# SwiGLU blocks: the rank of the copies and sums that empty a block's four banks

## The chip, the cores and the metric

The kernel runs on one core of a Trainium2 chip. The metric is device time in microseconds; of several executions the median is taken. In the profile's words TensorE is PE (its weight loads are PEld), VectorE is DVE, ScalarE is ACT, GpSimd is POOL and SyncE, which issues the transfers, is SP. L750 is line 750 of the kernel before.

## What is computed

An encoder of two layers on 256 tokens of width 1024, in float32. Each layer has a SwiGLU half-step, an attention stage, a second SwiGLU half-step and a gated embedding. The change is in the SwiGLU half-steps. D_FF is 2816.

```python
def rms_norm(x, g):
    xf = x.astype(jnp.float32)
    y = xf * lax.rsqrt(jnp.mean(xf * xf, axis=-1, keepdims=True) + EPS) * g.astype(jnp.float32)
    return y.astype(x.dtype)

def swiglu(h, w_in, w_out):
    gate, up = jnp.split(h @ w_in, 2, axis=-1)
    return (jax.nn.silu(gate) * up) @ w_out
...
    for i in range(DEPTH):
        x = x + 0.5 * swiglu(rms_norm(x, norm_ffn1[i]), ffn1_w_in[i], ffn1_w_out[i])
...
        x = x + 0.5 * swiglu(rms_norm(x, norm_ffn2[i]), ffn2_w_in[i], ffn2_w_out[i])
...
    return x
```

## The kernel before

Every float32 operand is held as two parts, a rounded one ("hi") and the remainder ("lo"), and a product is made of three matmuls: hi by hi, hi by lo, lo by hi. Weights are loaded as raw tiles of 128x1024 (wraw, four buffers). Weights.piece casts half a tile on ScalarE to whi (L236, or L238 with the norm's gain in it), and the remainder wlo is made on VectorE (L243, L245); whi and wlo have eight buffers each. When a tile's last remainder is made, its raw buffer is free and SyncE loads the next tile.

A SwiGLU half-step (ffn) runs over eleven blocks of 256 columns, numbered 0 to 10. Block 0 is made in another way. For blocks 1 to 10, columns(j) takes four banks at once, two of the kind mm (gate), one tp and one op (up), and runs 64 matmuls over four weight tiles. Each bank holds 128 columns of the block for all 256 tokens: hi by hi in its left half, the two mixed products in its right half. Then product(j, kc), once for each half kc of the block, empties a gate bank and an up bank: ScalarE copies the left halves (L742, L744), VectorE adds the right halves (gate_sum, L750, and other_sum, L757). The gate is multiplied by 1/rms (L752), goes through silu on ScalarE (L761), times up on VectorE (L766), and is split into hi and lo (pth by L458 on ScalarE, ptl by L466 on VectorE). Behind the columns of each block, and ahead of the next block's, come output units (OUT_BEHIND, out_unit): three or four times six matmuls of 512 columns into four banks of another kind, acc. The last four output parts (OUT_LEFT) come at the end.

The order of all engines' instructions is fixed when the program is built. A planner, Pace, holds a time for each engine and adds a cost for each instruction that it places. Work that waits for a result is entered with pace.at(time, function, engine, rank). When the planner's time reaches it, it goes on the engine's list of due work, and Pace.check takes the lowest rank first. Weight remainders have rank 5; casts of weights are placed by Weights.pump whenever the planner's ScalarE and VectorE are nearly idle. Banks and scratch buffers (sq, two of them) are given back at planned times. So a change of rank moves other work too, in all later stages.

Two more steps matter below. setup (L519 to L529) prepares the table of position biases: three small VectorE operations, a matmul into an op bank (L524), its copy on VectorE (L527), and a transfer to device memory on SyncE (L529). It is due at the planner's time 30 and then waits until an sq buffer and an op bank are free. zero_pads (L548) fills the zero columns of the keys and values on ScalarE, due at 40 with rank 9. The attention stage (mixers) makes queries and keys, normalises each head (L854 to L884), turns them with four transposes into the bank tp (L438), and goes on with scores and values, in an order that the planner finds step by step.

Of the kernel before, what the change touches and what calls it, by code (L numbers as in the profile page):

```python
# [19 lines left out]
DM, S, DEPTH, HD = 1024, 256, 2, 64  # L20
# [277 lines left out]
def encoder(ctx: ExitStack, tc, ins, out):  # L298
# [14 lines left out]
    pace = Pace()  # L313
# [6 lines left out]
    def can(kind):  # L320
        return slots[kind][turn[kind]] <= pace.now
# [10 lines left out]
    def give(tile, t=0.0):  # L332

        kind, k, _ = owner.pop(id(tile))
        slots[kind][k] = t
# [5 lines left out]
    def scratch(kind):  # L341
        return take(kind, sm.tile([P, 512], F32, tag=kind, name=kind, bufs=2))
# [109 lines left out]
    def parts(hi, lo, src, n, scale=None, bank=None, then=None, ready=None, prio=1):  # L452

        cell = {}

        def high():
            if scale is None:
                nc.scalar.copy(hi, src)  # L458
            else:
                nc.scalar.activation(hi, src, AF.Copy, scale=scale)  # L460
            cell["hi"] = pace.act(n, ready, scale=scale is not None)
            pace.at(cell["hi"], low, "dve", prio)

        def low():
            if scale is None:
                nc.vector.tensor_tensor(out=lo, in0=src, in1=hi.bitcast(F32), op=ALU.subtract)  # L466
            else:
                nc.vector.scalar_tensor_tensor(out=lo, in0=src, scalar=scale, in1=hi.bitcast(F32), op0=ALU.mult, op1=ALU.subtract)
            cell["lo"] = pace.dve(n, cell["hi"], scale=scale is not None)
            if bank is not None:  # L470
                give(bank, cell["lo"])
            if then:
                then(cell["lo"])
        ready = pace.done() if ready is None else ready
        pace.at(ready, high, "act", prio)
        return cell
# [159 lines left out]
    def ffn(a, ids, first=False):  # L636
# [8 lines left out]
        def slot(j):  # L645
            if j not in hT:
                hT[j] = take_pt()
            return hT[j]
# [59 lines left out]
        def columns(j):  # L708

            kinds = ("mm", "mm", "tp", "op")  # L710
            pace.until(lambda: all(max(slots[kind]) <= pace.now for kind in kinds))
            banks = [bank(kind) for kind in kinds]
            for c in range(4):
                ks = (2 * c, 2 * c + 1)
                pace.until(lambda: all(a.cell[t][k].get("lo") for t in range(2) for k in ks))
                wh, wl = W.get(ids_in[j][c])
                r = max(W.when[ids_in[j][c]], *(a.cell[t][k]["lo"] for t in range(2) for k in ks))
                every = [(k, n) for k in ks for n in range(4)]
                step = COLUMN_GROUP
                for g in range(0, 8, step):  # L720
                    for lower in range(2):
                        for k, n in every[g:g + step]:
                            x2 = xhl[:, k, :, :].rearrange("p u q -> p (u q)")
                            o = slice(512 * (k % 2) + P * n, 512 * (k % 2) + P * (n + 1))
                            if lower:
                                mm(banks[n][:, S:], wl[:, o], x2[:, :S], False, k == KD - 1)
                            else:
                                mm(banks[n], wh[:, o], x2, k == 0, False, r)
                            pace.check()
                W.used(ids_in[j][c])  # L730
                pace.check()
            for kc in range(2):
                product(j, kc, banks[kc], banks[2 + kc])

        def product(j, kc, g_ps, u_ps):
            pace.until(lambda: can("sq") and "r" in has)
            gu = scratch("sq")
            g, u = gu[:, :S], gu[:, S:]
            p0 = pace.done()

            def gate():
                nc.scalar.copy(g, g_ps[:, :S])  # L742
                t1 = pace.act(S, p0)
                nc.scalar.copy(u, u_ps[:, :S])  # L744
                t2 = pace.act(S, p0)
                pace.at(t1, lambda: gate_sum(t1), "dve", 0)
                pace.at(t2, lambda: other_sum(t2), "dve", 1)

            def gate_sum(t1):
                nc.vector.tensor_tensor(out=g, in0=g_ps[:, S:], in1=g, op=ALU.add)  # L750
                give(g_ps, pace.dve(S, t1))
                nc.vector.tensor_tensor(out=g, in0=g, in1=rms_b, op=ALU.mult)  # L752
                t3 = pace.dve(S, has["r"])
                pace.at(t3, lambda: act(t3), "act", 1)

            def other_sum(t2):
                nc.vector.tensor_tensor(out=u, in0=u_ps[:, S:], in1=u, op=ALU.add)  # L757
                give(u_ps, pace.dve(S, t2))

            def act(t1):  # L760
                nc.scalar.activation(g, g, AF.Silu)  # L761
                t2 = pace.act(S, t1, sbuf=True)
                pace.at(t2, lambda: prod(t2), "dve", 1)

            def prod(t2):
                nc.vector.tensor_tensor(out=u, in0=u, in1=g, op=ALU.mult)  # L766
                t3 = pace.dve(S, t2)
                split(t3)

            def split(t3):  # L770
                if j not in hT and not can("pt"):
                    pace.at(pace.now + 0.1, lambda: split(t3))
                    return
                hh, hl = slot(j)
                made[j, kc] = parts(hh[:, kc, :], hl[:, kc, :], u, S, ready=t3, then=lambda end: give(gu))
            pace.at(p0, gate, "act", 1)

        def out_unit(j, kc, t):
            if not acc:
# [456 lines left out]
```

## Time and profile before

| | us |
|---|---|
| median of 3 runs | 1029.19 (1029.05 to 1029.32) |
| profiled execution | 1029.5 |
| its span | 1027.7 |

| engine | busy us | share of the span | instructions |
|---|---|---|---|
| TensorE, matmuls | 1018.9 | 99% | 5466 |
| TensorE, weight loads | 875.6 | 85% | 5466 |
| VectorE | 765.4 | 74% | 1578 |
| ScalarE | 687.7 | 67% | 1438 |
| GpSimd | 34.0 | 3% | 38 |

How to read it: the span runs from the first to the last instruction of the program; the time of the execution is a little longer. Matmuls are pipelined, so that one of 512 columns lasts some 0.39 us while the next begins 0.23 us after it: distances between starts tell more than durations. A wait is put down to the engine and line that ended it last. By the chain of waits, 88% of the span is TensorE's.

### The profile page before, as it was taken

The page shows a single profiled execution, that of the slowest core. Times are in us where ns is not written, and L with a number is a line of the kernel's source. Part 1 is how long each engine was busy: PE and PEld are TensorE (multiplying, and loading weights), DVE is VectorE, ACT ScalarE, POOL GpSimd, SP SyncE. Part 2 cuts the span into 40 slices and gives each one's busy share as a digit, 9 for nine tenths or more (in the row PEclk, how much of TensorE's full clock was granted, in tenths as well). Part 3 has the DMA queues.
Part 4 walks back from the last instruction along what each step waited for, and adds up shares of the span by engine and source line. Part 5 has one row for each costly group of instructions (what it writes and reads, how often), then busy time and mean ns, then how long its engine had stood idle before and what let it go on. Part 6 is the DMA issues. An engine that isn't in the chain of part 4 may idle for free.

```text
span 1027.7 us, 15622 instructions
## 1 busy us (share of the span) xinstructions
PE 1018.9 (99%) x5466; PEld 875.6 (85%) x5466; DVE 765.4 (74%) x1578; ACT 687.7 (67%) x1438; POOL 34.0 (3%) x38
## 2 busy tenths in 40 slices
PE   9999999999999999999999999999999999999998
PEld 7788888879888888888888888888888888888887
DVE  6685874899887757847887478578998786578575
ACT  7775764778877646736886366467788775467464
POOL 0000000120100000000000000001110000000000
PEclk9999999999999999999999999999999999999999
DMA  8655764466435536745665457536664366366261
GB/s 296 222 204 165 230 206 156 147 230 209 150 119 201 177 114 211 234 150 170 235 193 180 145 172 258 165 132 209 206 195 132 120 208 219 102 228 231 97 207 62
DMA packets 55911, 187.30 MB, mean 182 GB/s; under 512 B 6502, under 2 KB 10854, under 8 KB 55832
## 3 DMA queue, kind: packets, MB, share of 16 engines
q1 hardware_dynamic: 55832, 186.30, 54.5%
q8 instruction: 43, 0.70, 0.3%
q14 instruction: 36, 0.29, 0.1%
HBM read 185.19 MB, written 1.08 MB: 181 GB/s over the span
## 4 chain that ended last, share of the span: by engine, by line
PE 88%; DVE 4%; ACT 3%; DMA 2%; issue 1%; POOL 1%; SPq 0%; ACTq 0%; DVEq 0%
PE acc L401 37%; PE mm L401 25%; PE op L401 12%; PE tp L401 10%; DVE wlo L245 2%; DMA wraw<-in_ffn_in_dram 2%; PE tp L438 2%; ACT whi L238 1%; POOL hrs L866 1%; PE op L438 1%; DMA wraw<-in_qkv_dram 0%; DVE kal L466 0%; PE acc L438 0%; DVE hss L862 0%; SPq L209 0%
## 5 line engine op out<-in xcount | busy, mean ns | idle before, releaser
L245 DVE SCALAR_TENSOR_TENSOR wlo<-wraw,gains,whi 128x512 fp32r<-128x512 f32 (+1 forms) x464 | 318.8, 737 | 52.7 <-ACT whi L238 49.8
L238 ACT ACTIVATE whi<-wraw,gains 128x512 fp32r<-128x512 f32 (+1 forms) x464 | 301.2, 707 | 65.2 <-DMA wraw<-in_ffn_in_dram 41.3
L401 PE MATMUL mm<-xhl,whi 128*128 128x512 f32 x640 | 200.2, 394 | 0.3 <-DVE sq L750 0.3
L243 DVE TENSOR_TENSOR wlo<-wraw,whi 128x512 fp32r<-128x512 f32 x216 | 140.3, 686 | 25.0 <-ACT whi L236 18.4
L236 ACT CAST whi<-wraw 128x512 fp32r<-128x512 f32 x216 | 124.2, 617 | 50.8 <-PE op L401 24.9
L401 PE MATMUL acc<-whi,pth 128*128 128x512 f32 x352 | 137.8, 391 | 0.0
L401 PE MATMUL acc<-wlo,pth 128*128 128x512 f32 x352 | 137.5, 390 | 0.0
L401 PE MATMUL acc<-whi,ptl 128*128 128x512 f32 x352 | 137.0, 389 | 0.0
L401 PE MATMUL mm<-xhl,wlo 128*128 128x256 f32 x640 | 127.8, 281 | 0.0
L401 PEld LDWEIGHTS mm<-xhl,whi 128*128 128x128 f32 x640 | 112.2, 189 | 17.7 <-DVE sq L750 0.9
L401 PE MATMUL op<-xhl,whi 128*128 128x512 f32 x320 | 125.5, 392 | 0.5 <-DVE sq L527 0.5
L401 PE MATMUL tp<-xhl,whi 128*128 128x512 f32 x320 | 124.6, 389 | 0.3 <-DVE sq L757 0.3
L401 PEld LDWEIGHTS mm<-xhl,wlo 128*128 128x128 f32 x640 | 110.0, 190 | 12.5
L750 DVE TENSOR_TENSOR sq<-mm,sq 128x256 f32<-128x256 f32 x80 | 33.7, 421 | 115.5 <-ACT sq L742 115.4
L401 PE MATMUL acc<-whi,xhl 128*128 128x512 f32 (+1 forms) x384 | 115.5, 373 | 0.0
L742 ACT COPY sq<-mm 128x256 f32<-128x256 f32 x80 | 30.4, 380 | 94.5 <-PE mm L401 94.5
L401 PE MATMUL op<-xhl,wlo 128*128 128x256 f32 x320 | 90.6, 283 | 0.0
L401 PE MATMUL tp<-xhl,wlo 128*128 128x256 f32 x320 | 90.5, 283 | 0.0
L401 PEld LDWEIGHTS acc<-whi,xhl 128*128 128x128 f32 x384 | 70.7, 189 | 12.3 <-ACT whi L238 0.7
L401 PEld LDWEIGHTS acc<-whi,ptl 128*128 128x128 f32 x352 | 66.1, 188 | 14.0
L401 PEld LDWEIGHTS acc<-whi,pth 128*128 128x128 f32 x352 | 66.3, 188 | 12.5
L401 PEld LDWEIGHTS acc<-wlo,pth 128*128 128x128 f32 x352 | 66.3, 188 | 12.1
(153 smaller groups left out, 1576.2 us busy)
## 6 DMA issues: line engine op xcount, KB each, us to landing
wraw<-in_ffn_in_dram SPq DMA_DIRECT2D x172, 512.0 KB, 4.4
wraw<-in_ffn_out_dram SPq DMA_DIRECT2D x88, 512.0 KB, 4.7
wraw<-in_qkv_dram SPq DMA_DIRECT2D x36, 512.0 KB, 3.6
wraw<-in_wo_dram SPq DMA_DIRECT2D x16, 512.0 KB, 3.8
wraw<-in_gate_dram SPq DMA_DIRECT2D x16, 512.0 KB, 4.1
bias<-bias_d SPq DMA_DIRECT2D x32, 192.0 KB, 3.7
wraw<-in_ffn_in_dram SPq DMA_DIRECT2D x8, 256.0 KB, 5.7
wraw<-in_ple_dram SPq DMA_DIRECT2D x4, 512.0 KB, 4.5
```

Of the source, the lines that this page charges most:

```text
L236: nc.scalar.copy(hi[:, a:b], raw[:, a:b])
L238: nc.scalar.activation(hi[:, a:b], raw[:, a:b], AF.Copy, scale=g)
L243: nc.vector.tensor_tensor(out=lo[:, a:b], in0=raw[:, a:b], in1=hi[:, a:b].bitcast(F32), op=ALU.subtract)
L245: nc.vector.scalar_tensor_tensor(out=lo[:, a:b], in0=raw[:, a:b], scalar=g, in1=hi[:, a:b].bitcast(F32), op0=ALU.mult, op1=ALU.subtract)
L401: nc.tensor.matmul(ps, lhsT=lhsT, rhs=rhs, start=start, stop=stop)
L438: nc.tensor.transpose(tp[:, n * P:(n + 1) * P], src, ident)
L742: nc.scalar.copy(g, g_ps[:, :S])
L750: nc.vector.tensor_tensor(out=g, in0=g_ps[:, S:], in1=g, op=ALU.add)
L866: nc.gpsimd.tensor_tensor(out=rs[:, :nh], in0=ss[:, :nh], in1=half_t[:, :nh], op=ALU.pow)
```

## The change

In product, three ranks change and one step is split. The first step, gate (the copies on ScalarE), goes from rank 1 to 0. The up sum goes from rank 1 to 0, the same as the gate sum. The scaling by 1/rms no longer follows the gate sum in the same step; it is a step of its own, scaled, at rank 1, entered for the time at which the sum is done.

```diff
--- before.py
+++ after.py
@@ -744,11 +744,15 @@
                 nc.scalar.copy(u, u_ps[:, :S])
                 t2 = pace.act(S, p0)
                 pace.at(t1, lambda: gate_sum(t1), "dve", 0)
-                pace.at(t2, lambda: other_sum(t2), "dve", 1)
+                pace.at(t2, lambda: other_sum(t2), "dve", 0)
 
             def gate_sum(t1):
                 nc.vector.tensor_tensor(out=g, in0=g_ps[:, S:], in1=g, op=ALU.add)
-                give(g_ps, pace.dve(S, t1))
+                end = pace.dve(S, t1)
+                give(g_ps, end)
+                pace.at(end, scaled, "dve", 1)
+
+            def scaled():
                 nc.vector.tensor_tensor(out=g, in0=g, in1=rms_b, op=ALU.mult)
                 t3 = pace.dve(S, has["r"])
                 pace.at(t3, lambda: act(t3), "act", 1)
@@ -773,7 +777,7 @@
                     return
                 hh, hl = slot(j)
                 made[j, kc] = parts(hh[:, kc, :], hl[:, kc, :], u, S, ready=t3, then=lambda end: give(gu))
-            pace.at(p0, gate, "act", 1)
+            pace.at(p0, gate, "act", 0)
 
         def out_unit(j, kc, t):
             if not acc:
```

No instruction is added or removed. Line numbers below the split grow by four: the scaling is L756 in the changed kernel, the up sum L761, the product L770.

VectorE, the end of block 1 in layer 1's first half-step (sq_431 and sq_432 are the scratch of the two halves, wlo_429 a weight remainder). Before:

```order
L750 TENSOR_TENSOR sq_431<-mm_283,sq_431 128x256
L752 TENSOR_TENSOR sq_431<-sq_431,rms_b_152 128x256
L750 TENSOR_TENSOR sq_432<-mm_284,sq_432 128x256
L752 TENSOR_TENSOR sq_432<-sq_432,rms_b_152 128x256
L757 TENSOR_TENSOR sq_431<-tp_285,sq_431 128x256
L757 TENSOR_TENSOR sq_432<-op_286,sq_432 128x256
L766 TENSOR_TENSOR sq_431<-sq_431 128x256
L766 TENSOR_TENSOR sq_432<-sq_432 128x256
L245 SCALAR_TENSOR_TENSOR wlo_429<-wraw_375,gains_89,whi_428 128x512
```

Now:

```order
L750 TENSOR_TENSOR sq_431<-mm_283,sq_431 128x256
L245 SCALAR_TENSOR_TENSOR wlo_429<-wraw_375,gains_89,whi_428 128x512
L761 TENSOR_TENSOR sq_431<-tp_285,sq_431 128x256
L750 TENSOR_TENSOR sq_432<-mm_284,sq_432 128x256
L761 TENSOR_TENSOR sq_432<-op_286,sq_432 128x256
L756 TENSOR_TENSOR sq_431<-sq_431,rms_b_152 128x256
L756 TENSOR_TENSOR sq_432<-sq_432,rms_b_152 128x256
L770 TENSOR_TENSOR sq_431<-sq_431 128x256
L770 TENSOR_TENSOR sq_432<-sq_432 128x256
L245 SCALAR_TENSOR_TENSOR wlo_429<-wraw_375,gains_89,whi_428 128x512
```

All four sums come ahead of the first scaling, and half of a weight tile's remainder has come in between. On ScalarE, the cast of that tile's second half now stands between the two silus.

TensorE, the start of block 2's columns, before (op_488 is the bank of setup's matmul):

```order
L401 MATMUL acc_436<-whi_381,pth_366 128x512
L401 MATMUL acc_436<-wlo_382,pth_366 128x512
L401 MATMUL acc_436<-whi_381,ptl_367 128x512
L524 MATMUL op_488<-qn_117,rb_116 16x512
L401 MATMUL mm_501<-xhl_151,whi_396 128x512
L401 MATMUL mm_502<-xhl_151,whi_396 128x512
L401 MATMUL tp_503<-xhl_151,whi_396 128x512
L401 MATMUL op_504<-xhl_151,whi_396 128x512
```

TensorE, the end of the output units ahead of block 5's columns, now:

```order
L401 MATMUL acc_433<-whi_855,pth_822 128x512
L401 MATMUL acc_433<-wlo_856,pth_822 128x512
L401 MATMUL acc_433<-whi_855,ptl_823 128x512
L524 MATMUL op_970<-qn_117,rb_116 16x512
L401 MATMUL acc_434<-whi_855,pth_822 128x512
L401 MATMUL acc_434<-wlo_856,pth_822 128x512
L401 MATMUL acc_434<-whi_855,ptl_823 128x512
L401 MATMUL mm_988<-xhl_151,whi_859 128x512
L401 MATMUL mm_989<-xhl_151,whi_859 128x512
L401 MATMUL tp_990<-xhl_151,whi_859 128x512
L401 MATMUL op_991<-xhl_151,whi_859 128x512
```

The setup's matmul has moved from ahead of block 2 to ahead of block 5, three matmuls before the end of the output units. Its copy (L527) moved with it on VectorE and stands behind the first of block 4's two product remainders; its transfer (L529) moved on SyncE from place 27 to place 44.

VectorE, the end of block 3's columns. Before:

```order
L245 SCALAR_TENSOR_TENSOR wlo_779<-wraw_727,gains_89,whi_778 128x512 x2
L750 TENSOR_TENSOR sq_793<-mm_668,sq_793 128x256
L752 TENSOR_TENSOR sq_793<-sq_793,rms_b_152 128x256
L750 TENSOR_TENSOR sq_794<-mm_669,sq_794 128x256
L752 TENSOR_TENSOR sq_794<-sq_794,rms_b_152 128x256
L757 TENSOR_TENSOR sq_793<-tp_670,sq_793 128x256
L757 TENSOR_TENSOR sq_794<-op_671,sq_794 128x256
L766 TENSOR_TENSOR sq_793<-sq_793 128x256
L766 TENSOR_TENSOR sq_794<-sq_794 128x256
```

Now:

```order
L245 SCALAR_TENSOR_TENSOR wlo_757<-wraw_708,gains_89,whi_756 128x512 x2
L245 SCALAR_TENSOR_TENSOR wlo_772<-wraw_723,gains_89,whi_771 128x512
L750 TENSOR_TENSOR sq_785<-mm_658,sq_785 128x256
L761 TENSOR_TENSOR sq_785<-tp_660,sq_785 128x256
L245 SCALAR_TENSOR_TENSOR wlo_772<-wraw_723,gains_89,whi_771 128x512
L750 TENSOR_TENSOR sq_786<-mm_659,sq_786 128x256
L761 TENSOR_TENSOR sq_786<-op_661,sq_786 128x256
L756 TENSOR_TENSOR sq_785<-sq_785,rms_b_152 128x256
L756 TENSOR_TENSOR sq_786<-sq_786,rms_b_152 128x256
```

The last half tile of weight remainders now comes after the first gate and up sums, and the scalings after all four sums.

In the attention stage the order of TensorE changes from the second group of head transposes on. Counted in the order, 36 matmuls stood between the first and the second group and 30 between the second and the third; now it is 39 and 36. The second layer's stage changes in the same way.

## Rows read from the trace of the kernel before

**Rows 1.** The page's first two sections: busy time of each engine; TensorE's granted clock by slices.
```profile
PE 1018.9 (99%) x5466; PEld 875.6 (85%) x5466; DVE 765.4 (74%) x1578; ACT 687.7 (67%) x1438; POOL 34.0 (3%) x38
...
PEclk9999999999999999999999999999999999999999
```

**Rows 2.** The view of waits, TensorE's weight loads: total us, times, longest us.
```profile
PEld op L401 <- DVE sq L527: 0.9, 1, 0.9
PEld mm L401 <- DVE sq L750: 0.9, 2, 0.6
...
PEld tp L401 <- DVE sq L757: 0.6, 1, 0.6
```

**Rows 3.** The chain that ended last: start us, us, what.
```profile
82.18 5.47 PE acc L401 x24
```

**Rows 4.** Timeline of TensorE, 35 to 39: start us, us, engine, line, operation.
```profile
35.47 0.39 PE L401 MATMUL acc<-whi,ptl 128*128 128x512 f32 x1
35.79 1.03 PE L524 MATMUL op<-qn,rb 34*16 34x512 f32 x2
36.74 0.73 PE L401 MATMUL mm<-xhl,whi 128*128 128x512 f32 x2
...
38.18 0.50 PE L401 MATMUL op<-xhl,whi 128*128 128x512 f32 x1 [0.47 <-DVE sq L527]
38.51 0.62 PE L401 MATMUL mm<-xhl,whi 128*128 128x512 f32 x2
```

**Rows 5.** Timeline of TensorE, 69 to 72 us.
```profile
69.25 0.39 PE L401 MATMUL acc<-whi,ptl 128*128 128x512 f32 x1
69.50 0.50 PE L401 MATMUL mm<-xhl,whi 128*128 128x512 f32 x1
...
71.09 0.50 PE L401 MATMUL tp<-xhl,whi 128*128 128x512 f32 x1 [0.29 <-DVE sq L757]
...
71.76 0.62 PE L401 MATMUL mm<-xhl,whi 128*128 128x512 f32 x2
```

**Rows 6.** Timeline of VectorE, 69 to 71 us.
```profile
69.03 0.42 DVE L750 TENSOR_TENSOR sq<-mm,sq 128x256 f32<-128x256 f32 x1
69.48 0.42 DVE L752 TENSOR_TENSOR sq<-sq,rms_b 128x256 f32<-128x256 f32 x1
...
70.62 0.42 DVE L757 TENSOR_TENSOR sq<-tp,sq 128x256 f32<-128x256 f32 x1
70.95 0.41 DVE L757 TENSOR_TENSOR sq<-op,sq 128x256 f32<-128x256 f32 x1
```

**Rows 7.** Timeline of VectorE, 37 to 39 us.
```profile
37.23 0.23 DVE L519 SCALAR_TENSOR_TENSOR gqk<-gains 128x2 f32<-128x2 f32 x2
...
37.45 0.67 DVE L527 COPY sq<-op 16x512 f32<-16x512 f32 x1
38.05 1.39 DVE L245 SCALAR_TENSOR_TENSOR wlo<-wraw,gains,whi 128x512 fp32r<-128x512 f32 x2
```

**Rows 8.** Timeline of ScalarE, 50 to 68 us.
```profile
50.11 0.40 ACT L548 CAST kbh<-zero_t 64x256 fp32r<-64x256 f32 x1
...
64.28 3.84 ACT L238 ACTIVATE whi<-wraw,gains 128x512 fp32r<-128x512 f32 x6 [0.87 <-DMA wraw<-in_ffn_in_dram]
```

**Rows 9.** Timelines of VectorE and TensorE after block 4, 84 to 88 us.
```profile
84.19 0.41 DVE L757 TENSOR_TENSOR sq<-op,sq 128x256 f32<-128x256 f32 x1
...
87.48 0.61 PE L401 MATMUL mm<-xhl,whi 128*128 128x512 f32 x2
```

**Rows 10.** Timeline of TensorE in layer 1's attention stage, 222 to 227 us.
```profile
222.37 0.39 PE L401 MATMUL mm<-whi,xhl 128*128 128x512 f32 x1
223.17 0.63 PE L438 MATMUL tp<-ident,qn 128*128 128x128 f32 x4 [0.41 <-DVE qn L884]
...
226.15 0.39 PE L401 MATMUL mm<-whi,xhl 128*128 128x512 f32 x1
226.85 0.66 PE L438 MATMUL tp<-ident,qn 128*128 128x128 f32 x4 [0.31 <-DVE qal L468]
```

## The prediction

> **What bounds the kernel now.** I read the page first, then who waits, then the timelines of the places where TensorE waits. TensorE is busy for 99% of the span, VectorE 74%, ScalarE 67%, and the granted clock is at nine tenths or more in every slice, the 2.4 GHz level [rows 1]. A busy share doesn't show that an engine is at its rate, so look at its pace: in the chain of waits 24 matmuls of 512 columns take 5.47 us [rows 3], 228 ns each, and 512 columns at 2.4 GHz are 213 ns. There is nothing to win inside such a stretch; only the places where TensorE stands still count.
>
> The change is about releasing the four banks of a block earlier. So the question is where TensorE waits for a bank. The weight loads' waits answer it [rows 2]: in the whole program TensorE waits twice for the gate sums of line 750 (0.9 us together) and once for an up sum of line 757 (0.6 us). There are 40 blocks with 160 bank releases. In the usual block, as after block 4, the last sum starts at 84.19 and takes 0.41, and TensorE comes back to these banks at 87.48 [rows 9]: almost 3 us of cover, given by the 24 output matmuls between [rows 3]. An earlier release is worth nothing there.
>
> The three waits lie at one place, at 69 to 72 us, where block 4 starts while block 3's banks are still held [rows 5]. At the pitch of 0.23 the four first matmuls would start at 69.48, and the next at 70.39; the next starts at 71.76. The stall is 1.37 us. VectorE is the cause: the first sum only starts at 69.03, then each half's sum and scaling follow in pairs [rows 6], and ahead of them ScalarE has six weight casts in one row from 64.28 [rows 8].
>
> **The change, part by part.** No operation is added or removed; each engine has the same instructions in another order. Four terms follow.
>
> 1. The setup of the bias table leaves block 2's start. The step waits for a free scratch buffer and a free op bank in the planner's time, and in the changed order it comes three blocks later. At its old place it costs TensorE directly [rows 4]: after the matmul at 35.47 the next block would start at 35.69, and its fifth matmul at 36.60. The setup runs from 35.79 to 36.74, then op waits for the copy of line 527, and the fifth matmul is at 38.51. That is 1.91 us, of which the wait is about 0.64 and restarts 0.2.
>
> 2. The same setup now stands three matmuls ahead of block 5's columns. TensorE pays its run again, 35.69 to 36.74 with the restart, 1.05 to 1.2; I take 1.1. Does op wait again? After the setup come three output matmuls, then mm, mm, tp: six times 0.23, or 1.4 us before op is wanted. The copy takes 0.67 [rows 7] and stands on VectorE just behind the first product low of that block, which is done earlier, so I take no wait; the bound above is the old 0.64, the one below 0. Behind the copy queue one weight low and the second product low; their tiles are used a block later. The step's own transfer moves on SyncE's queue as well, past 17 of its transfers; it waits for line 527, and the loads behind it wait for that same low anyhow. Nothing.
>
> 3. The stall at block 4. TensorE arrives 1.91 earlier, at 69.48 - 1.91 = 67.57, which by itself would make the wait longer. Two things work against it. First, VectorE and ScalarE come earlier too. In block 1's evacuation the weight low that starts at 38.05 had the setup's four operations (37.23 to 38.05, 0.82) ahead [rows 7], and two product lows, 0.33 each by the distance below; now it has neither, but it waits for a silu that ScalarE does one weight cast (3.84 for six, 0.64 each [rows 8]) later. Net 0.8 earlier, and the next load of weights hangs on it. One zero pad of 0.40 [rows 8] falls behind block 2's copies. So these engines run 1.1 us ahead of before at block 3; between 0 and 1.2 is possible. Second, one weight low, 0.67 (half of the 1.39 of two [rows 7], less a small overlap), goes behind the sums. The first gate sum starts at 69.03 - 1.1 - 0.67 = 67.26; then, with 0.33 between starts that don't depend on each other (70.62 to 70.95) where a sum and its own scaling are 0.45 apart (69.03 to 69.48) [rows 6], the up sum at 67.60, a weight low at 67.93, the second gate sum at 68.60 and the second up sum at 68.93, ended 69.35. TensorE: mm at 67.70, mm at 69.05, tp 69.28, op 69.51, next 69.74 against 68.48 without a wait. The stall becomes 1.26: a gain of 0.1, between a loss of 1.0 (no lead) and a gain of 1.2.
>
> 4. The attention stage, twice. Nothing of the diff is in it, but the planner's clock starts it otherwise, and its matmuls come in another order. Of the four groups of transposes of normalised heads, the third waits 0.57 (223.17, where the pitch says 222.60), the fourth 0.47 (226.85 after 226.38) [rows 10]; these are what TensorE loses at the stage's start. In the changed order the third group stands nine matmuls later, 2.0 us; VectorE has one weight low more, 0.67, ahead of it. So this wait should go. The fourth hangs on a low that frees the bank and stays. I take 0.6 off, and give half back, since a whole stage has a new order and nothing says that every new place is a lucky one: 0.3 per layer, 0.6 in all; from a gain of 1.3 to a loss of 1.0 per layer, the size of the waits in these rows.
>
> The scaling as its own step costs the product chain at most two VectorE operations, 0.7 us. Its result is used by output units after the next block's columns, or, for the last block, after three output units and two more, well over the 3 us of [rows 9]: cover enough.
>
> **Sum**: -1.91 + 1.1 - 0.1 - 0.6 = -1.5 us. The profiled execution has 1029.5 us (span 1027.7, the rest around it), so 1028.0 in its terms; the median of the runs is 1029.19, 0.3 lower, and from it the forecast is **1027.7 us**. A measurement of this kernel can tell 0.2%, 2.06 us, from no change, so this counts as no change, near the edge to faster.
>
> **Rivals.**
> - *The late engines eat it.* If VectorE and ScalarE have no lead at block 3, because the loads land when they did, the new stall is 1.0 longer, and only the better order of the sums is left: -1.91 + 1.0 + 1.1 - 0.6, or 1028.8. For it: the engines wait for loads right there. Against: those loads hang on VectorE's lows, which move forward.
> - *Attention gains in earnest.* Both waits of [rows 10] go in both layers, with the small ones after them, 1.3 each: -0.9 - 2.6, or 1025.7. For it: the third group clearly comes later. Against: the fourth waits for a bank, not for the matmul before it.
> - *Slower by a new wait in attention.* The planner places the transposes and value products where it believes the tiles ready; it knows nothing of TensorE's real 0.5 us waits. Each place that is two matmuls too early costs what [rows 10] show, 0.5. From three such places per layer (1.5 each, against the 0.9 saved before) the kernel loses; at four in each it is -0.9 + 4.0, or 1032.3. Against: the stage of before, planned by the same rules, has two.
> - *No effect.* The setup's waits come back at block 5 and the stall stays: -1.91 + 1.1 + 0.64 + 0.2, or 1029.2.
> - *TensorE isn't the bound.* The Trainium skill (Perfetto Trace Analysis, Identifying the Most-Contended Engine) holds that matmul busy time misleads and asks for the busy share of weight loads. By that rule the 85% here would leave 15%, and a prompt release could give several per cent. The mechanism in rows: matmuls would have to be further apart than their columns need; were the 0.9 us by which the last bank is free earlier (two scalings of 0.45) exposed in all 40 blocks, it would give 36 us, 993. The pace of [rows 3] speaks against it.
>
> **How the numbers follow.** Forecast 55%, spread over 1026.8 to 1028.6, a third of it below 1027.1 where faster begins; late engines 17%; attention gains 15%; slower 7%; no effect 4%; TensorE unbound 2%. Faster: 17 + 15 + 2 = 34%; same: 38 + 17 + 4 = 59%; slower 7%. The range goes from 1025.4, just past the attention case, to 1029.9, which takes in the late engines with a lost wait or two; the slower case and the last are left out. The forecast's own range is 1026.8 to 1028.6.
>
> **What would show it.** In the changed profile: no setup and no wait of op at 36 to 38 us; the setup's two passes near 84 us with no wait behind them; a stall of about 1.3 us at 67 to 70, with the first sum near 67.3; banks in all later blocks free 3 us early as before; the third group of head transposes without a wait. TensorE's waits for line 750 elsewhere, a first sum still near 68 or later, or waits of over 1 us in attention would prove the steps wrong.

## The result, and the profile after

The changed kernel takes 1034.7 us in the median of 3 runs (1034.59 to 1036.36), against 1029.19 before: a ratio of 1.0058, interval 1.0045 to 1.0072. It is slower by 5.5 us, clear of the noise. The forecast was 1027.7 with a range to 1029.9, and "slower" had 7%.

The page still shows TensorE busy for 99%, nearly the same weight loads, and less of the chain that ended last on TensorE (88% before, 80% now):

```profile
PE 1019.1 (99%) x5466; PEld 874.6 (85%) x5466; DVE 759.6 (74%) x1578; ACT 682.3 (66%) x1438; POOL 33.7 (3%) x38
...
PE 80%; DVE 8%; ACT 6%; DMA 4%; issue 2%; SPq 1%; POOL 0%; ACTq 0%; DVEq 0%
```

The busy shares say nothing of where 5 us went. What tells it is the start of the same matmul in both timelines of TensorE, at the first matmul of a block or stage. All times are of the two profiled executions:

| first matmul of | before | after | difference | less the first row |
|---|---|---|---|---|
| block 1, layer 1 | 18.42 | 17.41 | -1.01 | 0 |
| block 3 | 54.23 | 51.31 | -2.92 | -1.91 |
| block 4 | 69.50 | 66.57 | -2.93 | -1.92 |
| block 5 | 87.48 | 85.47 | -2.01 | -1.00 |
| attention, layer 1 | 194.86 | 192.92 | -1.94 | -0.93 |
| second half-step, layer 1 | 320.21 | 322.08 | +1.87 | +2.88 |
| attention, layer 2 | 701.74 | 703.71 | +1.97 | +2.98 |
| second half-step, layer 2 | 827.10 | 832.13 | +5.03 | +6.04 |
| end of the span | 1027.65 | 1032.71 | +5.06 | +6.07 |

The first row, called the first mark below, is not the change: up to it both kernels run the same order, and over twelve profiled kernels this matmul starts anywhere from 17.41 to 19.47. In this pair of profiles the early blocks then gain 1.0 us, where 0.9 was forecast (step 3 below says how much of that is luck). Then attention loses 3.8 us in layer 1 and 3.1 in layer 2, where no line of the diff is. The half-steps and the gated embedding behind it neither gain nor lose.

The early part first. Timeline of TensorE after the change, at the three places of [rows 4, 5, 9]:

```profile
34.47 0.39 PE L401 MATMUL acc<-whi,ptl 128*128 128x512 f32 x1
34.70 0.62 PE L401 MATMUL mm<-xhl,whi 128*128 128x512 f32 x2
...
35.60 0.62 PE L401 MATMUL mm<-xhl,whi 128*128 128x512 f32 x2
...
66.57 0.39 PE L401 MATMUL mm<-xhl,whi 128*128 128x512 f32 x1
67.83 0.47 PE L401 MATMUL mm<-xhl,whi 128*128 128x512 f32 x1 [0.87 <-DVE sq L750]
...
83.39 0.39 PE L401 MATMUL acc<-whi,ptl 128*128 128x512 f32 x1
83.71 1.03 PE L524 MATMUL op<-qn,rb 34*16 34x512 f32 x2
84.67 0.50 PE L401 MATMUL acc<-whi,pth 128*128 128x512 f32 x1
```

Block 2 starts with no setup, at the pitch (the distance between starts where nothing waits) of 0.23. At block 4 the second matmul starts 1.26 after the first, a stall of 1.03, where it was 1.37. Ahead of block 5 the setup takes 84.67 - 83.62 = 1.05, and op does not wait for its copy afterwards. VectorE at block 4 [rows 6] does what the order said:

```profile
65.93 0.43 DVE L750 TENSOR_TENSOR sq<-mm,sq 128x256 f32<-128x256 f32 x1
66.27 0.41 DVE L761 TENSOR_TENSOR sq<-tp,sq 128x256 f32<-128x256 f32 x1
66.61 0.74 DVE L245 SCALAR_TENSOR_TENSOR wlo<-wraw,gains,whi 128x512 fp32r<-128x512 f32 x1
67.26 0.42 DVE L750 TENSOR_TENSOR sq<-mm,sq 128x256 f32<-128x256 f32 x1
67.60 0.41 DVE L761 TENSOR_TENSOR sq<-op,sq 128x256 f32<-128x256 f32 x1
```

Now attention. The view of waits for TensorE's weight loads (total us, times, longest us) has two rows that the view before had not, and the row of qal, the remainder that frees the bank tp, has grown from 1.4 to 2.1; L1011 is ScalarE's scaling of one half of a head's probabilities by the reciprocal sum (L1007 before):

```profile
PEld acc L438 <- ACT L L1011: 3.5, 4, 1.9
PEld tp L438 <- DVE qal L468: 2.1, 2, 1.1
PEld mm L438 <- ACT L L1011: 2.1, 2, 1.0
```

Transposes of probabilities wait for that scaling six times in these rows, and a seventh time for 0.3. The longest wait, in layer 1, as timelines of SyncE, ScalarE and TensorE:

```profile
239.36 0.43 SPq L1061 DMA_DIRECT2D ple<-in_pT_dram  x1
```
```profile
244.73 0.62 ACT L458 CAST oth<-ple 128x512 fp32r<-128x512 f32 x1 [2.12 <-DMA ple<-in_pT_dram]
245.26 0.50 ACT L1011 ACTIVATE L<-L,ri 128x256 f32<-128x256 f32 x1
```
```profile
243.85 0.30 PE L438 MATMUL tp<-ident,qn 128*128 128x128 f32 x1
245.81 0.66 PE L438 MATMUL acc<-ident,L 128*128 128x128 f32 x4 [1.67 <-ACT L L1011]
```

ScalarE stands still for 2.12 us in front of one cast, of the embedding's input pT, whose transfer SyncE issued at 239.36. The scaling stands behind that cast in ScalarE's order, so it starts at 245.26, and TensorE reaches its transposes 1.9 us too early. Before, the transfer was issued at 239.36 as well, but the cast stood later and waited for nothing:

```profile
245.68 0.62 ACT L458 CAST oth<-ple 128x512 fp32r<-128x512 f32 x1
```

The second kind, at 299 us: timelines of VectorE, ScalarE and TensorE.

```profile
294.07 1.41 DVE L245 SCALAR_TENSOR_TENSOR wlo<-wraw,gains,whi 128x512 fp32r<-128x512 f32 x2
295.40 0.68 DVE L466 TENSOR_TENSOR ptl<-mm,pth 128x512 fp32r<-128x512 f32 x1
296.00 0.47 DVE L981 CUSTOM_DVE_ANT_0 L<-mm,bias,minus_sink 128x256 f32<-128x256 f32 x1
```
```profile
297.25 0.51 ACT L1011 ACTIVATE L<-L,ri 128x256 f32<-128x256 f32 x1 [1.59 <-DVE ri L1005]
...
299.42 0.51 ACT L1011 ACTIVATE L<-L,ri 128x256 f32<-128x256 f32 x1 [0.24 <-DVE ri L1005]
```
```profile
298.60 0.60 PE L438 MATMUL tp<-ident,L 128*128 128x128 f32 x4
299.99 0.66 PE L438 MATMUL mm<-ident,L 128*128 128x128 f32 x4 [0.79 <-ACT L L1011]
```

Two groups of transposes stand back to back on TensorE, and the second one's scaling is only done at 299.93. Ahead of it on VectorE three lows (a low is the remainder of a cast, made on VectorE; 1.41 for two and 0.68) came before the logits. In all, the starts of TensorE lie later than the pitch says by more than 0.23 us at three places per attention stage before (1.29 and 1.26 us) and at five and six places after (4.57 and 3.73). That is 3.3 of the 3.8 us lost in layer 1 and 2.5 of the 3.1 in layer 2; the rest lies in smaller distances.

### The profile page after: what moved, and what is told of

It reads as the page before. It is cut to its first block, busy times and chain, and to the rows that moved or that the text cites. A ratio compares the mean times of both kernels' runs of the same rounds, so it can differ in the third digit from the quotient of the medians.

```text
span 1032.7 us, 15543 instructions
## 1 busy us (share of the span) xinstructions
PE 1019.1 (99%) x5466; PEld 874.6 (85%) x5466; DVE 759.6 (74%) x1578; ACT 682.3 (66%) x1438; POOL 33.7 (3%) x38
## 4 chain that ended last, share of the span: by engine, by line
PE 80%; DVE 8%; ACT 6%; DMA 4%; issue 2%; SPq 1%; POOL 0%; ACTq 0%; DVEq 0%
PE acc L401 33%; PE mm L401 24%; PE op L401 11%; PE tp L401 10%; DVE wlo L245 2%; DMA wraw<-in_ffn_in_dram 2%; ACT whi L238 1%; PE tp L438 1%; DVE wlo L243 1%; DMA ple<-in_pT_dram 1%; ACT L L989 1%; DVE ptl L466 1%; DVE L L981 1%; ACT L L1011 1%; PE op L438 1%
## 5 line engine op out<-in xcount | busy, mean ns | idle before, releaser
L238 ACT ACTIVATE whi<-wraw,gains 128x512 fp32r<-128x512 f32 (+1 forms) x464 | 303.7, 707 | 71.5 <-DMA wraw<-in_ffn_in_dram 41.4
L401 PEld LDWEIGHTS mm<-xhl,wlo 128*128 128x128 f32 x640 | 110.0, 190 | 12.4
L401 PEld LDWEIGHTS acc<-wlo,pth 128*128 128x128 f32 x352 | 66.3, 188 | 11.9
```

The source lines that it names most:

```text
L238: nc.scalar.activation(hi[:, a:b], raw[:, a:b], AF.Copy, scale=g)
L401: nc.tensor.matmul(ps, lhsT=lhsT, rhs=rhs, start=start, stop=stop)
```

## The experiments

Two measures are used. The time is the median, with the ratio to the kernel before run beside it (1028.75, 1029.03 and 1029.31 us in the three sessions). The ratio is worked out from all runs and not from the medians alone. The length of an attention stage is the distance from its first matmul to the first matmul of the next half-step, in the profiled execution: 125.35 and 125.36 us before, 129.17 and 128.42 after, for the same 716 matmuls.

**The change in all blocks but the last of a half-step.** With it, all engines have the order of before in attention.

```diff
-                pace.at(t2, lambda: other_sum(t2), "dve", 0)
+                pace.at(t2, lambda: other_sum(t2), "dve", 1 if j == NFB - 1 else 0)
...
-                pace.at(end, scaled, "dve", 1)
+                if j == NFB - 1:
+                    scaled()
+                else:
+                    pace.at(end, scaled, "dve", 1)
...
-            pace.at(p0, gate, "act", 0)
+            pace.at(p0, gate, "act", 1 if j == NFB - 1 else 0)
```

> The change in every block but the last of each half-step; in both attention stages every engine then has its instructions in the order of the kernel before. Theory A (the loss lies in the attention stage's new order, the blocks gain): the gain of the early blocks stays, the attention stages take what they took before, 1028.2 us, 1.0 under the kernel before. Theory B (the new ranks cost time in the blocks themselves): nine of ten blocks still have them, so 1034 us.

Measured: 1028.28 us, ratio 0.9992 (0.9983 to 1.0001). The stages take 125.30 and 125.31 us, and no transpose waits for the scaling. The whole view of waits of TensorE's matmuls is, apart from one wait of line 513 at the program's start:

```profile
PE mm L401 <- DVE sq L750: 1.3, 2, 0.9
PE tp L438 <- DVE qn L891: 0.9, 2, 0.4
PE tp L438 <- DVE qal L468: 0.5, 2, 0.3
```

So nine of the ten changed blocks cost nothing in attention; the loss comes with the last block. The other half of theory A, a gain of 1.0, is neither shown nor ruled out: the interval goes from 1.7 us faster to 0.1 slower. Less the first mark, the early gain was 0.33 at block 5, since the stall at block 4 was 1.7 in this execution.

**The mirror: the change in the last block alone** (the same edit with j != NFB - 1). The setup stays at block 2, and all engines have the order of after in attention.

> The mirror of the first experiment: the new ranks and the split in the last block of each half-step alone; all other blocks as before. The setup stays ahead of block 2, the blocks of the first half-step have the order of before up to the last one, and the attention stage has the changed kernel's order of matmuls. Theory A (the loss is the order that the planner finds for attention, whatever happens earlier): +3.8 in layer 1 and +3.1 in layer 2, nothing gained early, so before + 6.9: with 1028.75 for before, about 1035.6, and more than the changed kernel itself. Theory B (the loss comes from engines and loads that arrive earlier in attention than they did): no loss without the early gain, 1028.8. If it lies between, by the waits for the scalings on ScalarE that are there and those that are not.

Measured: 1034.98 us, ratio 1.0056 (1.0043 to 1.0069); the stages take 127.52 and 127.75 us. The last block alone brings the slowdown, with no early gain at all. In the profile, of 1033.75 us, the loss is two thirds of what was expected. In layer 1 the difference is the wait for pT, which costs TensorE 0.34 here and not 1.90. ScalarE's timeline has the same order as after, but the transfer landed 3.8 us after its issue at 240.77 and not 5.4:

```profile
243.52 0.52 ACT L458 CAST kbh<-tp 64x128 fp32r<-64x128 f32 x2
244.59 0.62 ACT L458 CAST oth<-ple 128x512 fp32r<-128x512 f32 x1 [0.55 <-DMA ple<-in_pT_dram]
```

**The transfer of pT at the start of the stage**, in the changed kernel. Only SyncE's order changes.

```diff
+        ple = [att.tile([P, DM], F32, tag=f"ple{t}", name="ple") for t in range(2)]
+        nc.sync.dma_start(out=ple[1][:, 512:].rearrange("q (k c) -> q k c", k=2), in_=ins["pT"][i])
...
-        ple = [att.tile([P, DM], F32, tag=f"ple{t}", name="ple") for t in range(2)]
...
-            nc.sync.dma_start(out=pr.rearrange("q (k c) -> q k c", k=2), in_=ins["pT"][i])
```

> The changed kernel; only the transfer of the layer's embedding input is issued at the start of the attention stage instead of in its middle, so it stands earlier on SyncE's queue and no other engine's order changes. Theory A1 (ScalarE stands at the cast of that input, and TensorE behind it, because the transfer lands late): the waits of 1.9 us in layer 1 and 0.6 us in layer 2 before the transposes go, 1032.2 us. Theory A2 (ScalarE is late for other work and only stands there by chance): the scaling that the transposes wait for is as late as now, 1034.5 us.

Measured: 1033.08 us, ratio 1.0040 (1.0027 to 1.0052); the stages take 128.18 and 127.43 us, 1.0 less each than after. ScalarE's cast no longer waits:

```profile
243.71 0.62 ACT L458 CAST oth<-ple 128x512 fp32r<-128x512 f32 x1
244.24 0.51 ACT L1013 ACTIVATE L<-L,ri 128x256 f32<-128x256 f32 x1
```

TensorE's wait of 1.9 there is gone, but only 1.0 came back in the length of the stage. Waits further on stay or grow (0.63 at 286.0, 1.03 at 298.9, 0.80 at 227.4). The cause is that of theory A1, at less than its price: the time lies between the two. By this run the transfer is a quarter to a third of the loss, and the rest stays with the order. The mirror shows that its share varies: with a wait of 0.34 there, layer 1 took 1.65 less than after.

**The setup alone moved**, in the kernel before, to the planner's time 84:

```diff
-    pace.at(30.0, lambda: when(setup, "sq", "op"))
+    pace.at(84.0, lambda: when(setup, "sq", "op"))
```

> The kernel before; only the setup of the bias table is due at the planner's time 84 instead of 30, which puts it ahead of block 6. Ranks and the order of the attention stages are those of before. If moving the setup is all of the early gain: 1.9 saved at block 2, 1.05 to 1.7 paid at block 6, 1028.4 to 1029.0 us. If the banks of block 3 matter, TensorE comes to them 1.9 earlier with the old order of sums and waits about 1 us longer there: 1029.2 to 1029.9 us.

Measured: 1030.07 us, ratio 1.0009 (1.0000 to 1.0018): no gain. That is 0.9 us slower, a little above the ranges of both theories (0.2 to 0.8 faster than before, and up to 0.7 slower), and its interval takes in the second. Less its first mark, block 3 starts 1.92 earlier than before. At block 5 it is 1.34, so the start of block 4, where the banks of block 3 are still held, took 0.6 back. The setup, which now starts at 118.64, costs 1.04 up to the next block's first matmul and 0.3 behind it, which leaves nothing. Attention stays at 125.29 and 125.33 us. The profile measures the setup's terms one by one.

**Two ranks alone, without the split**, in the kernel before:

```diff
-                pace.at(t2, lambda: other_sum(t2), "dve", 1)
+                pace.at(t2, lambda: other_sum(t2), "dve", 0)
...
-            pace.at(p0, gate, "act", 1)
+            pace.at(p0, gate, "act", 0)
```

> The kernel before with the two ranks alone (copies and up sum at 0); the scaling stays in one step with the gate sum. The attention stage gets a third order, neither that of before nor that of the change. Theory A: the time is set by what waits this order happens to have, anywhere from 1028 to 1035 us, and the difference to before lies between the landmarks of the attention stages. Theory B: the loss comes with the ranks, so 1032 us or more with the difference spread over the blocks.

Measured: 1038.51 us, ratio 1.0088 (1.0074 to 1.0101). This is a third order of attention, and the stages take 129.04 and 130.60 us; the early blocks gain 0.5. Theory A had the place right, with 3.7 and 5.2 us lost in the two stages, but the time lies 3.5 above its range. TensorE's waits for the same scaling (here L1007) are longer, and some are at other places:

```profile
PE mm L438 <- ACT L L1007: 5.7, 4, 2.6
```

**A margin in the planner**, in the changed kernel: transposes of probabilities go 1.0 us after the planner believes them ready.

```diff
-            if nT < nqk and nT in ahead and len(ahead[nT]) == 2 and ahead[nT][1] <= pace.now and kind and can("pt"):
+            if nT < nqk and nT in ahead and len(ahead[nT]) == 2 and ahead[nT][1] + 1.0 <= pace.now and kind and can("pt"):
```

> The changed kernel, with one number more: the planner places the transposes of a head's probabilities 1.0 us after the time at which it believes the scaled probabilities ready. Theory C (the planner is too optimistic about the scalings on ScalarE; TensorE reaches the transposes about 1 us too early): the waits of 1.9 and 1.0 in layer 1 and 1.0 and 0.6 in layer 2 for the scaling on ScalarE shrink to below 0.5 each, 2.5 to 3.5 us in all, so about 1031 with 1028.75 for before, and no such wait over 0.5 is left in the view of waits. Theory D (any new order of the stage is a new draw, the margin changes only which one): waits of 0.5 to 2 us at other places, a sum between that of before and 5 us per layer, 1028 to 1038. The margin may also cost by itself, since later transposes make later value products and hold the probability tiles longer: up to 1 us per layer.

Measured: 1028.82 us, ratio 1.0003 (0.9993 to 1.0013). The whole loss is gone, more than the 2.5 to 3.5 us of theory C: the stages take 125.51 and 125.59 us, and beside the wait of line 513 TensorE's matmuls wait only for

```profile
PE tp L438 <- DVE qal L468: 1.3, 2, 0.7
PE tp L438 <- DVE qn L888: 0.8, 2, 0.4
PE acc L401 <- ACT whi L238: 0.2, 1, 0.2
```

By itself this speaks for theory C: the planner is too early with this kind of matmul.

**The same margin on the first experiment** (the change in all blocks but the last).

> The change in every block but the last (the first experiment, 1028.28) with the same margin of 1.0 us on the transposes. By theory C the margin helps here little, since this attention stage has few waits for the scaling (0.24 per layer), and costs little: 1027.5 to 1028.5. By theory D it is a new draw and may be anything from 1027 to 1036; a time over 1030 shows that the margin is no cure.

Measured: 1033.77 us, ratio 1.0043 (1.0031 to 1.0056), the stages 127.77 and 127.59 us. The margin that saved some 6 us in the changed kernel costs some 5 here, far outside theory C's range. No transpose waits for the scaling any more, but a value product waits for the cast of its probabilities, 1.27 us beyond the pitch in each layer, over half of what the stage loses:

```profile
PE op L401 <- ACT pth L458: 2.2, 2, 1.1
```

**A second margin, of 1.0 us on the value products**, on the changed kernel and on the first experiment:

```diff
-            if nv < nT and ahead[nv][2].get("lo", 1e9) <= pace.now and (nv >= NHA or have("va")) and (nv % 2 or can("op")):
+            if nv < nT and ahead[nv][2].get("lo", 1e9) + 1.0 <= pace.now and (nv >= NHA or have("va")) and (nv % 2 or can("op")):
```

> The changed kernel with the margin of 1.0 us on the transposes of the probabilities (as in e6_margin, 1028.82 beside 1029.03 for before) and one of 1.0 us on the value products as well. Theory C2 (each wait in attention is a product that the planner places too early; a margin on a kind of product removes the waits of that kind and costs nothing): the stage stays as in e6_margin, within 0.5 us per layer, 1028.3 to 1029.5, with no wait for ScalarE's casts or scalings over 0.3. Theory D (any new order is a new draw): waits at other places, 1028 to 1036.

> The change in all blocks but the last, with both margins; with the first margin alone (e7_last_margin, 1033.77) TensorE waited 1.27 us per layer for the cast of a probability tile ahead of a value product, and the stage lost 2.4 and 2.2. Theory C2: that wait goes with the second margin; the rest of the loss, some 1 us per layer, stays or goes with it: 1028.5 to 1031. Theory D: a new draw, 1028 to 1036, with the loss at waits of another kind.

Measured: 1032.44 us, ratio 1.0033 (1.0020 to 1.0045), stages 126.95 and 127.38; and 1030.85 us, ratio 1.0017 (1.0008 to 1.0026), stages 126.60 and 126.64. The first lies 3 us above the range of theory C2, the second inside the ranges of both theories. In both, the waits of the kinds aimed at are gone or below 0.3, and others have come: for the bank of logits (line 981) in the first, for the residual's update (line 1137) in the second. The first:

```profile
PE mm L401 <- DVE nm L981: 0.7, 2, 0.3
PE tp L438 <- ACT L L1011: 0.4, 2, 0.2
```

The second:

```profile
PE tp L438 <- DVE x_sb L1137: 1.7, 2, 1.0
```

**Transposes of the normalised heads 0.6 us later**, beside the margin of 1.0 on the probabilities, in the changed kernel:

```diff
-                with_bank("tp", t4 + 0.8, lambda: finish(qn, t4))
+                with_bank("tp", t4 + 1.4, lambda: finish(qn, t4))
```

> The changed kernel with the margin of e6_margin and the transposes of the normalised heads placed 0.6 us later. The four waits left in e6_margin are of this kind: 0.60 and 0.76 in layer 1, 0.57 and 0.85 in layer 2. Theory C2: the two for the normalised heads (0.60, 0.57) go, those for the bank (0.76, 0.85) shrink or stay: 1 to 2.5 us below e6_margin, 1026.5 to 1028, the fastest of all. Theory D: the order of the whole stage shifts, and what comes is a draw, 1027 to 1036.

Measured: 1033.45 us, ratio 1.0050 (1.0037 to 1.0062), stages 129.25 and 129.51, in a profiled execution of 1036.79. The four waits aimed at are gone, but the next transposes of heads wait 0.56 for their bank in each layer, and a value product waits 1.75 us in each layer for a low that stands ahead on VectorE:

```profile
PE op L401 <- DVE otl L466: 3.5, 2, 1.7
```

**All orders together.** Eight orders of attention have been profiled, each the greedy planner's answer to a slightly different start or rule:

| order of | layer 1, us | layer 2, us |
|---|---|---|
| before | 125.35 | 125.36 |
| the change with one margin | 125.51 | 125.59 |
| first experiment, both margins | 126.60 | 126.64 |
| the change, both margins | 126.95 | 127.38 |
| first experiment, one margin | 127.77 | 127.59 |
| the change | 129.17 | 128.42 |
| two ranks alone | 129.04 | 130.60 (clock fell once) |
| the change, later heads, one margin | 129.25 (clock fell once) | 129.51 (clock fell once) |

A fall of the granted clock to the 1.2 GHz level makes three of these lengths some 1.5 us longer, an estimate from the windows in the last section. The order explains most of the spread. The three kernels that have that of before lie within 0.1 us of each other in both layers. The three that have that of the change take 127.5 to 129.2 and 127.4 to 128.4, in part because one wait of this order hangs on when a transfer lands. A margin removes the waits it is aimed at, each time, yet it also changes all that follows, and whether the sum gets better can't be read from the rule. Theory C and its wider form C2 missed their ranges in the first experiment with one margin, in the change with both and with the later heads, so as a cure they fall. Theory D, that a new order is a new draw, kept to its range each time, but its ranges of 8 to 10 us were hard to miss. No version tried is faster than before by more than a measurement can tell. The first experiment and the single margin are equal to it.

## Why the prediction was wrong

**What bounds the kernel** was right: TensorE's pace holds, and only places where it stands still count. An earlier release of banks showed only at block 4; in all later blocks the two timelines keep their distance. The rival that TensorE is not the bound falls: the weight loads' share is 85% in both kernels, 5 us apart, so it does not tell them apart, and the losses above are for the most part places where TensorE stands still, not a slower pace.

**Step 1** (setup leaves block 2, -1.91): measured -1.91 at block 3, and -1.92 with the setup alone moved. Right.

**Step 2** (setup paid again, +1.1): 1.05 in the timeline; with the restart and what follows, up to block 5, 1.26. No second wait of op. Right.

**Step 3** (stall 1.37 to 1.26): measured 1.03. Counted from each kernel's first mark, the first gate sum was forecast at 67.26 - 18.42 = 48.84 and came at 65.93 - 17.41 = 48.52. The sums stand where the step put them, but that the size came out so close is luck. Seven more profiled kernels have the same order up to block 5. There the stall is 0 once (the single margin), 1.6 to 1.8 five times and 2.1 once: in six of seven it is longer than the 1.37 of before. That 1.37 is one case too: the mirror, with the order of before there, has 1.9. In all eight the first gate sum comes 36.6 to 37.6 us after a ScalarE cast (L238) that waits for a weight load; that cast comes 10.4 us after the first mark where the stall is 0, 11.4 in the profile after, and 11.9 to 12.4 in the others. So by these timelines, though by no test, the stall hangs in the main on when that load lands, which is the mechanism of the rival "the late engines eat it", at less than its price of 1.0.

The three steps together, forecast -0.9, gave -1.0 by block 5 in the profile after. Over the eight kernels it is -2.0 once, -1.0 once, -0.2 to -0.4 five times, and +1.6 once, where the granted clock fell at block 4. A gain of 1 us by the new order of the early blocks is therefore not shown.

**Step 4 failed**: "I take 0.6 off, and give half back", 0.3 gained per layer, with bounds of -1.3 to +1.0, "the size of the waits in these rows". Measured: +3.8 and +3.1. The single wait it named did go: the third group of head transposes no longer waits. The fourth's wait rose from 0.47 to 0.71, and the second group, which did not wait before, now waits 0.68 beyond the pitch. The second, third and fourth group after the change:

```profile
214.71 0.63 PE L438 MATMUL tp<-ident,qn 128*128 128x128 f32 x4 [0.52 <-DVE qn L888]
...
223.40 0.60 PE L438 MATMUL tp<-ident,qn 128*128 128x128 f32 x4
...
227.30 0.66 PE L438 MATMUL tp<-ident,qn 128*128 128x128 f32 x4 [0.55 <-DVE qal L468]
```

The large losses are of a kind that the stage of before never shows, at the probabilities' scaling. The bounds came from two waits in the stage of before. But that stage is one outcome of the planner, the best of the eight seen, so its waits bound nothing from above. A bound for "another order" has to come from all products placed by belief: the transposes and value products of 16 heads in two layers are 64 places. In the eight orders single waits there reach 2.8 us, and a stage takes up to 5 us more than before, a fall of the clock included. The profile of the change also has the sign that the prediction set against itself, a wait of over 1 us in attention.

**The rival that came true** is "slower by a new wait in attention". Its mechanism is the one found, a product placed too early by the planner's belief. Its price, 0.5 per place and four places per layer, was too low for the single place (up to 1.9) and for the sum (3.8 against 2.0), and its 7% was too little: it was argued down by "the stage of before, planned by the same rules, has two".

What is shown, by the first experiment and its mirror: the last block's ranks and split switch the order of attention, and that order carries the loss. What is shown in part: one wait comes from the pT transfer, about 1.0 us per layer when the transfer alone is moved. That the planner is too early at the probabilities' transposes is borne out by the single margin, which takes these waits away; but it changes the order behind them too, so it does not show their price by itself. Only read from the timeline, and not tested alone, is that the wait at 299 us comes from the weight lows ahead of the logits.

## What to carry to other kernels

Where a planner or scheduler fixes the order, an edit of ranks moves every stage that comes after it. Compare the order there as well, and price a reshuffled stage by the spread over several orders, not by the waits of the one at hand. A step's local gain of 1 us or less is worth nothing as long as it can reseed a stage whose outcomes lie 4 us apart; keep the late stages' order fixed (here, leave the last block as it was) and measure the local change by itself. Take more than one profile before a local gain is believed: the same early order gave anything from 0.2 to 2.0 us here, and a loss where the clock fell.

## What was not expected of the hardware

**A stall can be paid twice.** In the profiled execution of the last experiment the granted clock falls at the end of the wait for the low. TensorE's windows (start and end, then us; busy of TensorE and of weight loads first, PEclk third from the end):

```profile
296.00:300.00 4.00, 1.90 (x12) 1.46 (x11) 3.93 (x11) 4.00 (x12) 0.00 (x0) 0.95 0.04 12
300.00:304.00 4.00, 4.00 (x18) 3.63 (x18) 1.73 (x3) 0.79 (x2) 0.00 (x0) 0.62 0.68 251
304.00:308.00 4.00, 4.00 (x22) 3.42 (x21) 1.49 (x3) 1.71 (x3) 0.00 (x0) 1.00 0.01 3
```

And its timeline of TensorE:

```profile
296.60 0.28 PE L401 MATMUL op<-pth,vbl 128*128 128x256 f32 x1
296.71 0.28 PE L401 MATMUL op<-pth,vbh 128*128 128x256 f32 x1
...
299.70 0.58 PE L401 MATMUL op<-pth,vbh 128*128 128x256 f32 x1 [1.75 <-DVE otl L466]
300.08 0.41 PE L401 MATMUL op<-pth,vbl 128*128 128x256 f32 x1
300.30 0.41 PE L401 MATMUL op<-pth,vbh 128*128 128x256 f32 x1
```

Ahead of the fall TensorE was busy for 1.90 of 4 us. Then 256 columns take 0.22 and not 0.11 to 0.12, the 1.2 GHz level, for some 3 us: 4 x (1 - 0.62) = 1.5 us more. It happens in both layers of this execution, once with two ranks alone (at the end of the wait of 2.76 in layer 2) and once with both margins on the first experiment (at block 4). It does not come with every execution: of the five runs of the last experiment the profiled one, with a mean clock of 0.996, took 1036.79 us, and three with a mean clock of 0.999 took 1033.28 to 1033.45. The wait of 1.9 in the changed kernel did not bring it in the execution profiled: the clock there stayed at 1.00.

**The same transfer lands at different times.** From the issue of pT to the start of a cast that waits for it, 5.4 us passed in layer 1 and 4.1 in layer 2 of the changed kernel, and 3.8 in both layers of the mirror; over all eight such casts in the profiled kernels it is 3.8 to 5.7. The planner's code counts on 4.0. An order that puts a cast right at its expected landing makes ScalarE, and all that stands behind, carry that spread.
